# Low parts of K's weights by an accumulating DMA, and K's third group as Strassen pairs

## The chip, the cores and the metric

The kernel runs on one core of one Trainium2 chip. The metric is device time in microseconds (us), from three runs.

## The reference, cut to what matters

A two-layer decoder trunk over 256 tokens, model width 2048, fp32. After the first layer's output `x`, one projection gives the keys and values of three head groups, which the second layer reads:

```python
def shared_kv(x, g, w_kv):
    B, S, _ = x.shape
    parts = split_cols(rmsnorm(x, g) @ w_kv, [DIL_W] * (2 * len(DIL_CONFIG)))   # K0 V0 K1 V1 K2 V2, 2048 columns each
    return [t.reshape(B, S, DIL_HEADS, DIL_DH) for t in parts]
```

So the change lies in one matrix product: 256 tokens by 2048, times 2048 by 12288, in six blocks of 2048 columns. The rest (projections, retention, attention, gates, norms) stays as it is.

## The kernel before, in words

Every fp32 product is made from rounded halves. A tile of 128 x 1024 weights is loaded into `raw`; ACT (ScalarE) writes its rounded high part `wh` (line L97), DVE (VectorE) the rest, `wl = raw - wh` (L98); TensorE multiplies both with the activations' halves. `wh` and `wl` have five buffers each (`SPL = 5`), given out in turn, `raw` has six. SP issues the loads; POOL (GpSimd) issues the DMAs to and from scratch in DRAM (`spill`, `fetch`).

K and V are made in what is called the mixed stage here. K has 12 chunks of 512 columns, each by `dense_cols`: two column halves `i`, in each four weight tiles `j`, in each tile eight times a matmul over 512 columns with `wh` (L315) and one over 256 columns with `wl` (L317): channels come out on the partitions. V is made in pairs of chunks by `strassen`, seven products of quarter blocks instead of eight. A pair is a generator of 28 steps; a step makes one product tile: DVE adds blocks of weights where needed (L361), ACT and DVE split the result, and TensorE does six matmuls over 512 columns (L371 to L373), tokens on the partitions. After certain tiles of K, `weave(n)` runs n steps of the generators in `woven`: (2, 2, 1, 0) after the four tiles of a half and 3 after its eviction. In the stage K's sums live in one accumulator, `acc0`; Strassen's in `acc1` and `acc2`. Small jobs wait in `pending`, and `step()` runs a piece of one of them.

The order on each engine is set by a list scheduler when the kernel is built, with a priority for each instruction; `tc.high_priority(AHEAD)` moves instructions to the front. Each engine then runs its own list strictly in that order and waits on semaphores. The pieces of lists below are its result.

The combinations of activations that Strassen needs (`combine`) are made beside K's first chunk, in which nothing is woven. The scaled activations `yk` (for K and V) and later `yb` (for layer 2) share their source tiles `src`, which stay in SBUF through the stage.

Of the kernel before, what the change touches and what calls it, by code (L numbers as in the profile page):

```python
# [9 lines left out]
F32 = mybir.dt.float32  # L10
F32R = mybir.dt.float32r
AF = mybir.ActivationFunctionType
ALU = mybir.AluOpType
# [8 lines left out]
AHEAD = 100  # L22
# [6 lines left out]
def yoco_trunk_kernel(  # L29
# [8 lines left out]
    pe, act, dve, pool, sp = nc.tensor, nc.scalar, nc.vector, nc.gpsimd, nc.sync  # L38
# [10 lines left out]
    woven = deque()  # L49

    def big_tile(dt=F32):
        return big.tile([P, 4, 256], dt, name="big")
# [16 lines left out]
    def flat(t):  # L69
        return t.rearrange("p a b -> p (a b)")  # L70
# [13 lines left out]
    def acc_tile(name=None):  # L84
        if name is None:
            name = ("acc0", "acc1")[0 if woven else turns["acc"] % 2]
            turns["acc"] += 1
        return psum.tile([P, 2, 2, S], F32, name=name)
# [16 lines left out]
    pending = deque()  # L105
# [9 lines left out]
    def drain():  # L115
        while pending:
            step()

    def weave(n=1):
        for _ in range(n):  # L120
            while woven:
                try:
                    next(woven[0])
                    break
                except StopIteration:
                    woven.popleft()
# [122 lines left out]
    def split_weights(raw, g, k0, n, wh, wl):  # L249
        with tc.high_priority(AHEAD):  # L250
            if g is None:
                split(wh, wl, raw)
                return
            w = 1024 // n
            for i in range(n):
                cs = slice(i * w, (i + 1) * w)
                gs = gain[:, g, k0 + i:k0 + i + 1]
                act.activation(wh[:, cs], raw[:, cs], AF.Copy, scale=gs)
                dve.scalar_tensor_tensor(wl[:, cs], raw[:, cs], gs, wh[:, cs].bitcast(F32), ALU.mult, ALU.subtract)

    def weights(src, g, k0, n, keep=False):
        raw = wraw.tile([P, 1024], F32, name="raw")
        sp.dma_start(out=raw, in_=src)
        if keep:
            wh, wl = flat(big_tile(F32R)), flat(big_tile(F32R))
        else:
            wh = wspl.tile([P, 1024], F32R, name="wh")
            wl = wspl.tile([P, 1024], F32R, name="wl")
        split_weights(raw, g, k0, n, wh, wl)
        w = 1024 // n  # L270
        return [(wh[:, i * w:(i + 1) * w], wl[:, i * w:(i + 1) * w]) for i in range(n)]

# [30 lines left out]
        for i in range(2):  # L303
            evict(i, ps[i])

    def dense_cols(xs, w, c, evict, g=None):
        for i in range(2):
            ps = acc_tile()
            for j in range(4):
                part = xs[j]  # L310
                for a, (wh, wl) in enumerate(weights(w[c, i, j], g, 4 * j, 4)):
                    first, last = j == 0 and a == 0, j == 3 and a == 3
                    for ct in range(2):
                        cs = slice(ct * P, (ct + 1) * P)
                        pe.matmul(ps[:, ct].rearrange("p h s -> p (h s)"), lhsT=wh[:, cs], rhs=xhl(part, a),  # L315
                                  start=first, stop=False, skip_group_check=True)
                        pe.matmul(ps[:, ct, 0, :], lhsT=wl[:, cs], rhs=xh(part, a),  # L317
                                  start=False, stop=last, skip_group_check=True)
                    if a % 2:
                        step()  # L320
                weave((2, 2, 1, 0)[j])
            if woven:
                with tc.high_priority(2 * AHEAD):
                    evict(i, ps)
                weave(3)
            else:
                evict(i, ps)

# [102 lines left out]
    def dense(xs, w, c, g=None, order=(0, 1, 2, 3), both=None, after=None):  # L431
        pt = acc_tile().rearrange("p t h s -> p t (h s)")
        ps = [pt[:, t, :] for t in range(2)]
        n = 4 * len(order)
        k = 0
        late = []

        def row_part(t, part, a, wh, wl, first, last):
            ts = slice(t * P, (t + 1) * P)
            pe.matmul(ps[t], lhsT=xh(part, a)[:, ts], rhs=wh, start=first, stop=False)  # L440
            pe.matmul(ps[t], lhsT=xh(part, a)[:, ts], rhs=wl, start=False, stop=False)  # L441
            pe.matmul(ps[t], lhsT=xl(part, a)[:, ts], rhs=wh, start=False, stop=last)  # L442

        for j in order:
            if len(order) > 4 and j == order[-1]:
                drain()
            part = xs[j]
            for u in range(2):
                keep = both is not None and k >= both
                for a, (wh, wl) in enumerate(weights(w[c, j, u], g, 4 * j + 2 * u, 2, keep), 2 * u):  # L450
                    first, last = k == 0, k == n - 1
                    k += 1
                    row_part(0, part, a, wh, wl, first, last)
                    if keep:
                        late.append((1, part, a, wh, wl, first, last))
                    else:
                        row_part(1, part, a, wh, wl, first, last)
                    step()
                    if len(order) > 4 and k % 2 == 0:
                        step()  # L460
        if after is not None:
            after(ps[0])
        for args in late:
            row_part(*args)
        return ps
# [22 lines left out]
        dense_cols(*job[:3], evict, *job[3:])  # L488
        return h, l

    def cols_scaled(b, *job):
        o = big_tile()

        def evict(i, ps):
            fold(half(o, i), ps)
            if b is not None:
                scale_half(o, i, b)

        dense_cols(*job[:3], evict, *job[3:])
        return o  # L500

    def scale_half(o, i, b):
# [7 lines left out]
    def rows_scaled(ps, r):  # L510
        o = rows(big_tile())
        for t in range(2):
            act.activation(o[:, t, :], ps[t], AF.Copy, scale=r[:, t:t + 1])
        return o
# [230 lines left out]
    def turn_cols(xr, yt):  # L745
        for i in range(2):
            ps = bank()
            for ct in range(2):
                for t in range(2):
                    cs = slice((2 * i + ct) * P, (2 * i + ct + 1) * P)  # L750
                    pe.transpose(ps[:, ct * S + t * P:ct * S + (t + 1) * P], xr[:, t, cs], ident)
            act.copy(half(yt, i), ps)
            yield
# [24 lines left out]
    def spill(t):  # L778
        d = dram.tile([P, 1024], F32, name=f"spill{turns['spill']}")
        turns["spill"] += 1  # L780
        pool.dma_start(out=d, in_=t)
        return d

    def fetch(d):
        t = big_tile()
        pool.dma_start(out=flat(t), in_=d)
        return t

    n_m, n_x = Norm("m"), Norm("x")
    ms = SplitCols(memt, GM)  # L790
    xs = SplitCols(xt, GA)
# [26 lines left out]
    mk0 = big_tile()  # L818
    dense_cols_first(ms, memt, w_mk[0, 0:1], lambda i, ps: fold(half(mk0, i), ps))
    pending.append(stats_m())  # L820
    mk1 = cols_scaled(None, ms, w_mk[0], 1)
    drain()
    for i in range(2):
        scale_half(mk1, i, n_m.b)
# [29 lines left out]
    yk, yb = Scaled(GK), Scaled(GB)  # L854
# [20 lines left out]
        dve.memset(o, v)  # L875
        setattr(n_y, f, o)

    comb = {}

    def make_y():  # L880
        ss = small.tile([P, 2], F32, name="ss")
        dve.tensor_reduce(ss, part, AX.X, ALU.add)
        n_y.rstd(ss)
        yield
        for c in range(4):
            for t in range(2):
                act.activation(x1[c][:, t, :], x1[c][:, t, :], AF.Copy, scale=n_y.r[:, t:t + 1])
            yield
            yk.src[c] = yb.src[c] = big_tile()
            yield from turn_cols(x1[c], yk.src[c])  # L890
            yield from yk.start(c)

    pending.append(make_y())
    mk_b = [spill(flat(cols_scaled(n_m.b, ms2, w_mk[1], c))) for c in range(2)]
    mv_b = [spill(rows_scaled(dense(ms2, w_mv[1], c), n_m.r).rearrange("p t c -> p (t c)")) for c in range(2)]
    drain()
    kd, vd = {}, {}

    def done(p):
        def f(o1, o2):  # L900
            for n, o in ((2 * p, o1), (2 * p + 1, o2)):
                vd[n // 4, n % 4] = spill(o.rearrange("p t c -> p (t c)"))
        return f

    pending.append(combine(yk.raw, comb))
    for i in range(3):
        for hg in range(4):
            kd[i, hg] = spill(flat(cols_plain(yk, w_kc, 4 * i + hg)))
            if not kd.keys() - {(0, 0)}:
                drain()  # L910
                for p in range(6):
                    woven.append(strassen(yk, comb, w_vs[p], done(p)))
    while woven:
        weave()

# [11 lines left out]
        yield  # L927

    for j in range(4):
        pending.append(yb.start(j))  # L930
    mix = SplitMix()
    for c in range(2):
# [163 lines left out]
```

## Time and profile before

| | |
|---|---|
| runs | 1897.88, 1902.02, 1902.39 us; median 1902.02 |
| profiled execution, its own time | 1899.93 us |
| its span, first to last instruction | 1898.2 us |
| TensorE busy, share of the span | 1875.5 us, 99% |
| VectorE | 1317.7 us, 69% |
| ScalarE | 985.8 us, 52% |
| granted TensorE clock | 1.00 in every stage |

A matmul's listed duration (400 ns for 512 columns) overlaps with its neighbours', so what one costs is read from the distance between starts in the timeline, and a "99% busy" TensorE can still hold short waits. A tile's name without its buffer number (`wl`, `big`) stands for all its buffers.

### The profile page before, as it was taken

The numbers are of one execution on the slowest core, as the hardware profiler recorded it, in microseconds if no ns is written. First come the engines' busy times: TensorE is split into PE (matmuls) and PEld (weight loads), VectorE is DVE, ScalarE is ACT, GpSimd is POOL, SyncE is SP. The second block draws the span as 40 slices with busy tenths as digits, with TensorE's granted clock in tenths as the row PEclk, the third lists the DMA queues.
The fourth block names the chain that finished last, engine by engine and source line by source line (L and its number), as shares of the span: only waits on it lengthen the run. The fifth ranks groups of instructions, "written<-read, shape, count | busy, mean of one in ns | idle before, by whom it ended". The sixth has DMA issues, their size and how long they took to land.

```text
span 1898.2 us, 25963 instructions
## 1 busy us (share of the span) xinstructions
PE 1875.5 (99%) x9988; PEld 1604.6 (85%) x9988; DVE 1317.7 (69%) x1571; ACT 985.8 (52%) x1288; POOL 47.5 (3%) x88
## 2 busy tenths in 40 slices
PE   8999999999999999999999999999999999999997
PEld 7888888888888888888888888788889898888886
DVE  7766765665564757899999999866657475656643
ACT  6554445444454645555655556554545454545543
POOL 1000000000000000000000000000000000000000
PEclk9999999999999999999999999999999999999999
DMA  9654565565676666575766667666655556566462
GB/s 304 234 167 157 162 202 180 168 202 184 215 253 208 196 213 212 201 251 192 244 211 222 240 203 256 233 222 210 202 187 181 187 160 218 165 207 220 151 199 100
DMA packets 112588, 385.25 MB, mean 203 GB/s; under 512 B 12385, under 2 KB 18577, under 8 KB 112465
## 3 DMA queue, kind: packets, MB, share of 16 engines
q1 hardware_dynamic: 102784, 349.22, 56.5%
q0 software_dynamic: 9536, 34.37, 5.0%
q8 instruction: 78, 1.28, 0.3%
q14 instruction: 46, 0.37, 0.1%
q10 hardware_dynamic: 144, 0.01, 0.0%
HBM read 364.68 MB, written 18.87 MB: 202 GB/s over the span
## 4 chain that ended last, share of the span: by engine, by line
PE 93%; DVE 2%; issue 2%; ACT 1%; DMA 1%; SPq 0%; POOL 0%; ACTq 0%; POOLq 0%; DVEq 0%
PE acc L315 33%; PE acc L317 17%; PE acc L440 9%; PE acc L441 9%; PE acc L442 9%; PE acc L371 4%; PE acc L372 4%; PE acc L373 4%; DVE wl L98 1%; PE att L102 1%; PE att L103 1%; PE att L101 1%; PE acc L298 1%; ACT wh L97 1%; PE att L714 1%
## 5 line engine op out<-in xcount | busy, mean ns | idle before, releaser
L98 DVE TENSOR_TENSOR wl<-raw,wh 128x1024 fp32r<-128x1024 f32 (+1 forms) x642 | 769.3, 1209 | 461.8 <-ACT wh L97 459.9
L97 ACT CAST wh<-raw 128x1024 fp32r<-128x1024 f32 (+1 forms) x642 | 660.4, 1040 | 673.8 <-PE acc L315 263.6
L315 PE MATMUL acc<-big,wh 128*128 128x512 f32 x2752 | 983.5, 400 | 5.6 <-DVE big L221 2.4
L317 PE MATMUL acc<-big,wl 128*128 128x256 f32 x2752 | 771.3, 280 | 0.8 <-DVE wl L98 0.8
L315 PEld LDWEIGHTS acc<-big,wh 128*128 128x128 f32 x2752 | 517.8, 188 | 127.7 <-DVE big L470 3.1
L317 PEld LDWEIGHTS acc<-big,wl 128*128 128x128 f32 x2752 | 520.2, 189 | 5.0 <-DVE wl L98 1.1
L440 PE MATMUL acc<-wh,big 128*128 128x512 f32 x744 | 291.6, 392 | 0.0
L441 PE MATMUL acc<-wl,big 128*128 128x512 f32 x744 | 289.8, 390 | 0.0
L442 PE MATMUL acc<-wh,big 128*128 128x512 f32 x744 | 289.8, 390 | 0.0
L442 PEld LDWEIGHTS acc<-wh,big 128*128 128x128 f32 x744 | 139.7, 188 | 29.1
L440 PEld LDWEIGHTS acc<-wh,big 128*128 128x128 f32 x744 | 139.8, 188 | 28.2
L441 PEld LDWEIGHTS acc<-wl,big 128*128 128x128 f32 x744 | 139.8, 188 | 27.8
L371 PE MATMUL acc<-wh,big 128*128 128x512 f32 x336 | 133.2, 397 | 1.2 <-ACT wh L97 1.0
L372 PE MATMUL acc<-wl,big 128*128 128x512 f32 x336 | 131.7, 392 | 0.5 <-DVE wl L98 0.5
L373 PE MATMUL acc<-wh,big 128*128 128x512 f32 x336 | 131.6, 392 | 0.0
L97 ACT CAST wh<-big 128x1024 fp32r<-128x1024 f32 x72 | 75.5, 1049 | 72.5 <-DVE big L361 57.7
L98 DVE TENSOR_TENSOR wl<-big,wh 128x1024 fp32r<-128x1024 f32 x72 | 87.8, 1220 | 19.3 <-ACT wh L97 19.1
L371 PEld LDWEIGHTS acc<-wh,big 128*128 128x128 f32 x336 | 63.1, 188 | 17.1 <-ACT wh L97 1.7
L373 PEld LDWEIGHTS acc<-wh,big 128*128 128x128 f32 x336 | 63.1, 188 | 14.8
L372 PEld LDWEIGHTS acc<-wl,big 128*128 128x128 f32 x336 | 63.2, 188 | 11.8 <-DVE wl L98 1.0
L361 DVE TENSOR_TENSOR big<-big,raw 128x1024 f32<-128x1024 f32 x48 | 58.5, 1219 | 0.3
L98 DVE TENSOR_TENSOR big<-big 128x512 fp32r<-128x512 f32 (+1 forms) x54 | 43.4, 823 | 4.6 <-ACT big L97 3.2
(230 smaller groups left out, 1264.5 us busy)
## 6 DMA issues: line engine op xcount, KB each, us to landing
raw<-in_w_b_dram SPq DMA_DIRECT2D x160, 512.0 KB, 3.5
raw<-in_w_kc_dram SPq DMA_DIRECT2D x96, 512.0 KB, 4.4
raw<-in_w_vs_dram SPq DMA_DIRECT2D x96, 512.0 KB, 4.5
raw<-in_w_ac_dram SPq DMA_DIRECT2D x64, 512.0 KB, 3.5
raw<-in_w_ar_dram SPq DMA_DIRECT2D x64, 512.0 KB, 3.9
raw<-in_w_oa_dram SPq DMA_DIRECT2D x48, 512.0 KB, 3.5
raw<-in_w_ob_dram SPq DMA_DIRECT2D x48, 512.0 KB, 3.5
raw<-in_w_mv_dram SPq DMA_DIRECT2D x32, 512.0 KB, 3.5
```

Source lines behind the costliest of these rows:

```text
L97: act.copy(hi, src)
L98: dve.tensor_tensor(lo, src, hi.bitcast(F32), ALU.subtract)
L101: pe.matmul(o, lhsT=ah, rhs=bh, start=first, stop=False, skip_group_check=True)
L315: pe.matmul(ps[:, ct].rearrange("p h s -> p (h s)"), lhsT=wh[:, cs], rhs=xhl(part, a), start=first, stop=False, skip_group_check=True)
L317: pe.matmul(ps[:, ct, 0, :], lhsT=wl[:, cs], rhs=xh(part, a), start=False, stop=last, skip_group_check=True)
L361: f(*args)
L371: pe.matmul(ps, lhsT=h, rhs=wh[:, cs], start=first, stop=False, skip_group_check=True)
L372: pe.matmul(ps, lhsT=h, rhs=wl[:, cs], start=False, stop=False, skip_group_check=True)
L373: pe.matmul(ps, lhsT=l, rhs=wh[:, cs], start=False, stop=last, skip_group_check=True)
L440: pe.matmul(ps[t], lhsT=xh(part, a)[:, ts], rhs=wh, start=first, stop=False)
L441: pe.matmul(ps[t], lhsT=xh(part, a)[:, ts], rhs=wl, start=False, stop=False)
L442: pe.matmul(ps[t], lhsT=xl(part, a)[:, ts], rhs=wh, start=False, stop=last)
```

## The change

It has four parts. (1) While Strassen steps are woven in, a K tile's low part is no longer made by DVE: ACT writes `wh`, ACT writes `wl = -wh` (L272 of the changed kernel), and a DMA from POOL's queue adds the weights, read from DRAM once more, onto `wl` in SBUF (L273). (2) K's third group, four of the twelve chunks, becomes two more Strassen pairs; their output has tokens on the partitions, so each of their four chunks is turned by eight 128 x 128 transposes on TensorE (`turn_out`, a pending job) and then spilled. (3) The order: `combine` moves ahead into V's second chunk of layer 2's memory projection, the generators start with K's first chunk, eight K chunks run beside eight pairs, and the weaves become (4, 4, 3, 0) and 4. (4) `yk.src` is spilled and fetched again for `yb` behind the stage; one accumulator is named `acc2` early in the kernel.

```diff
-        split_weights(raw, g, k0, n, wh, wl)
+        if woven:
+            with tc.high_priority(AHEAD):
+                act.copy(wh, raw)
+                act.activation(wl, wh.bitcast(F32), AF.Copy, scale=-1.0)
+                pool.dma_start(out=wl, in_=src, accum_op=ALU.add)
+        else:
+            split_weights(raw, g, k0, n, wh, wl)
...
-                weave((2, 2, 1, 0)[j])
+                weave((4, 4, 3, 0)[j])
             if woven:
                 with tc.high_priority(2 * AHEAD):
                     evict(i, ps)
-                weave(3)
+                weave(4)
...
-    mk1 = cols_scaled(None, ms, w_mk[0], 1)
+    mk1 = cols_scaled(None, ms, w_mk[0], 1, name="acc2")
...
-            yk.src[c] = yb.src[c] = big_tile()
+            yk.src[c] = big_tile()
             yield from turn_cols(x1[c], yk.src[c])
+            yd.append(spill(flat(yk.src[c])))
             yield from yk.start(c)
...
+    for c in range(2):
+        if c == 1:
+            pending.append(combine(yk.raw, comb))
+        mv_b.append(spill(rows_scaled(dense(ms2, w_mv[1], c), n_m.r).rearrange("p t c -> p (t c)")))
...
+    def turn_out(o, key):
+        t = big_tile()
+        yield from turn_cols(o, t)
+        kd[key] = spill(flat(t))
...
-                vd[n // 4, n % 4] = spill(o.rearrange("p t c -> p (t c)"))
+                if n < 12:
+                    vd[n // 4, n % 4] = spill(o.rearrange("p t c -> p (t c)"))
+                else:
+                    pending.append(turn_out(o, (2, n % 4)))
...
-    pending.append(combine(yk.raw, comb))
-    for i in range(3):
+    for p in (0, 1, 6, 2, 3, 7, 4, 5):
+        woven.append(strassen(yk, comb, w_vs[p], done(p)))
+    for i in range(2):
         for hg in range(4):
             kd[i, hg] = spill(flat(cols_plain(yk, w_kc, 4 * i + hg)))
-            if not kd.keys() - {(0, 0)}:
-                drain()
-                for p in range(6):
-                    woven.append(strassen(yk, comb, w_vs[p], done(p)))
...
     for j in range(4):
+        yb.src[j] = fetch(yd[j])
         pending.append(yb.start(j))
```

What this does to the lists, at three places in the middle of the mixed stage. A row is a line of the code, an operation, the tile written, the tiles read, the width, and the kind of semaphore waited on. First TensorE, before: the end of one K tile (`wl_8601`), one Strassen step, and the start of the next K tile, `wl_8644`.

```order
L315 MATMUL acc0_8502<-big_5605,wh_8600 128x512
L317 MATMUL acc0_8502<-big_5605,wl_8601 128x256
L371 MATMUL acc1_6389<-wh_8631,big_6235 128x512 [waits Activation_49]
L372 MATMUL acc1_6389<-wl_8632,big_6235 128x512 [waits DVE_49]
L373 MATMUL acc1_6389<-wh_8631,big_6235 128x512
L371 MATMUL acc1_6389<-wh_8631,big_6235 128x512
L372 MATMUL acc1_6389<-wl_8632,big_6235 128x512
L373 MATMUL acc1_6389<-wh_8631,big_6235 128x512
L315 MATMUL acc0_8502<-big_5689,wh_8643 128x512 [waits Activation_49]
L317 MATMUL acc0_8502<-big_5689,wl_8644 128x256 [waits DVE_49]
L315 MATMUL acc0_8502<-big_5689,wh_8643 128x512
```

TensorE, after (L315, L317 and L371 to L373 are now L321, L323 and L377 to L379). The row just ahead of these is the last that reads the K tile `wl_8871`; its buffers are the ones that `wh_8951` and `wl_8952`, five tiles on, will get.

```order
L379 MATMUL acc2_6214<-wh_8929,big_6013 128x512
L377 MATMUL acc2_6214<-wh_8929,big_6013 128x512
L378 MATMUL acc2_6214<-wl_8930,big_6013 128x512
L379 MATMUL acc2_6214<-wh_8929,big_6013 128x512
L377 MATMUL acc1_6213<-wh_8939,big_6052 128x512
L378 MATMUL acc1_6213<-wl_8940,big_6052 128x512 [waits DVE_49]
L379 MATMUL acc1_6213<-wh_8939,big_6052 128x512
L377 MATMUL acc1_6213<-wh_8939,big_6052 128x512
L378 MATMUL acc1_6213<-wl_8940,big_6052 128x512
L379 MATMUL acc1_6213<-wh_8939,big_6052 128x512
L321 MATMUL acc0_8796<-big_5610,wh_8951 128x512 [waits Activation_49]
L323 MATMUL acc0_8796<-big_5610,wl_8952 128x256 [waits DMASW5_49]
```

The first use of `wl` now waits for a DMA of POOL's queue (DMASW) where it waited for DVE. Between the last read of the old owner and the first read of `wl_8952` stand eleven matmuls.

Second ACT, around the same K tiles; before, one copy for each tile:

```order
L97 CAST wh_8600<-raw_8598 128x1024 [waits DMAHW1_49,DVE_49,PE_49]
L97 CAST wh_8631<-raw_8622 128x1024 [waits DVE_49,PE_49,Activation_49]
L97 CAST wh_8643<-raw_8641 128x1024 [waits DMAHW5_49,PE_49,Activation_49]
L97 CAST wh_8665<-big_8626 128x1024 [waits PE_49,Activation_49]
L97 CAST wh_8675<-raw_8624 128x1024 [waits DMAHW4_49,PE_49,Activation_49]
L97 CAST wh_8685<-raw_8620 128x1024 [waits DMAHW2_49,PE_49,Activation_49]
```

and after, with the copy (L271) and the negation (L272) of the K tiles:

```order
L433 COPY big_8358<-acc2_6214 128x512 [waits DVE_49,PE_49]
L271 CAST wh_8951<-raw_8949 128x1024 [waits DMAHW6_49,DVE_49]
L272 ACTIVATE wl_8952<-wh_8951 128x1024 [waits DMASW0_49,Activation_49]
L97 CAST wh_8972<-raw_8908 128x1024 [waits DMAHW3_49,DVE_49,PE_49]
L97 CAST wh_8993<-raw_8984 128x1024 [waits DVE_49,PE_49]
L97 CAST wh_9003<-big_8988 128x1024 [waits PE_49]
L271 CAST wh_9015<-raw_9013 128x1024 [waits DMAHW2_49,PE_49]
L272 ACTIVATE wl_9016<-wh_9015 128x1024 [waits Activation_49]
```

Each K tile now has two rows on ACT, and other tiles' copies behind them. Third POOL, the same stretch; before it held only spills:

```order
L781 DMA spill19_8401<-big_7748 128x1024 [waits DMASW7_49,DVE_49]
L781 DMA spill18_8399<-big_7747 128x1024 [waits DMASW0_49,Activation_49]
L781 DMA spill20_8695<-big_8305 128x1024 [waits DMASW1_49,DVE_49]
L781 DMA spill23_9080<-big_8697 128x1024 [waits DMASW2_49,DVE_49]
L781 DMA spill22_9078<-big_8426 128x1024 [waits DMASW3_49,DVE_49]
```

and after, the accumulating DMAs (L273) stand between them in one list:

```order
L787 DMA spill25_8904<-big_8359 128x1024 [waits DMASW2_49,DVE_49]
L273 DMA wl_8871<-in_w_kc_dram 128x1024 [waits DMASW1_49,PE_49,Activation_49]
L787 DMA spill24_8902<-big_8358 128x1024 [waits DVE_49,Activation_49]
L273 DMA wl_8952<-in_w_kc_dram 128x1024 [waits DMASW0_49,DMASW5_49,PE_49,Activation_49]
L273 DMA wl_9016<-in_w_kc_dram 128x1024 [waits DVE_49,PE_49,Activation_49]
L787 DMA spill26_9089<-big_8512 128x1024 [waits DVE_49]
L273 DMA wl_9096<-in_w_kc_dram 128x1024 [waits DMASW6_49,PE_49,Activation_49]
```

There are 60 such DMAs in the stage; four of K's 64 tiles come after the last Strassen step and keep DVE's subtraction.

## Rows read from the trace of the kernel before

**Rows 1.** The page: span, busy time, share of the span and instructions of each engine.

```profile
span 1898.2 us, 25963 instructions
...
PE 1875.5 (99%) x9988; PEld 1604.6 (85%) x9988; DVE 1317.7 (69%) x1571; ACT 985.8 (52%) x1288; POOL 47.5 (3%) x88
```

**Rows 2.** Windows, 720 to 1227 us: busy us (instructions) by engine, clock, DMA share, GB/s.

```profile
720.00:1227.00 507.00, 504.89 (x2545) 423.81 (x2543) 470.19 (x453) 290.14 (x319) 12.79 (x24) 1.00 0.67 224
```

**Rows 3.** Waits, 717 to 1212 us: who waited for whom; total us, times, longest us.

```profile
ACT wh L97 <- DVE raw L361: 85.0, 22, 6.2
...
ACT wh L97 <- PE acc L373: 15.9, 20, 3.1
...
PEld acc L371 <- ACT wh L97: 1.7, 2, 0.9
...
PE acc L372 <- DVE wl L98: 0.5, 1, 0.5
```

**Rows 4.** Timeline of PE: start us, us, engine, line, operation, tiles, shape, count.

```profile
719.97 0.39 PE L315 MATMUL acc<-big,wh 128*128 128x512 f32 x1
...
1210.82 0.40 PE L371 MATMUL acc<-wh,big 128*128 128x512 f32 x1
...
1213.34 0.39 PE L373 MATMUL acc<-wh,big 128*128 128x512 f32 x1
...
1214.38 0.39 PE L315 MATMUL acc<-big,wh 128*128 128x512 f32 x1
...
1217.55 0.40 PE L315 MATMUL acc<-big,wh 128*128 128x512 f32 x1
...
1226.58 0.28 PE L317 MATMUL acc<-big,wl 128*128 128x256 f32 x1
```

**Rows 5.** Groups by line, 717 to 1212 us: count, busy us, mean ns, idle before.

```profile
L98 DVE TENSOR_TENSOR wl<-raw,wh 128x1024 fp32r<-128x1024 f32 x187 | 221.2, 1219 | 12.1 <-ACT wh L97 11.1
...
L97 ACT CAST wh<-raw 128x1024 fp32r<-128x1024 f32 x187 | 189.5, 1049 | 113.5 <-DVE raw L361 85.0 <-PE acc L315 9.1 <-PE acc L373 7.9
...
L361 DVE TENSOR_TENSOR big<-big,raw 128x1024 f32<-128x1024 f32 x48 | 58.5, 1219 | 0.3
...
L470 DVE TENSOR_TENSOR big<-acc,big 128x512 f32<-128x512 f32 x22 | 15.0, 684 | 1.2 <-ACT big L469 1.2
...
L416 DVE TENSOR_TENSOR big<-big,acc 128x512 f32<-128x512 f32 x15 | 9.5, 680 | 0.1
```

**Rows 6.** The chain that ended last, 630 to 640 us: start us, us, engine, line.

```profile
633.94 0.44 PE att L751 x4
```

**Rows 7.** Timeline of ACT in the stage before, 700 to 722 us.

```profile
703.85 1.05 ACT L97 CAST wh<-raw 128x1024 fp32r<-128x1024 f32 x1 [1.67 <-PE acc L442]
706.57 1.05 ACT L97 CAST wh<-raw 128x1024 fp32r<-128x1024 f32 x1 [1.67 <-PE acc L442]
709.29 1.05 ACT L97 CAST wh<-raw 128x1024 fp32r<-128x1024 f32 x1 [1.67 <-PE acc L442]
```

**Rows 8.** Groups by line and shape, the whole run: a plain copy and a scaled one.

```profile
L97 ACT CAST big<-sm 128x512 fp32r<-128x512 f32 x20 | 12.3, 616 | 11.4 <-DVE sm L470 11.4
...
L540 ACT ACTIVATE sm<-big 128x512 f32<-128x512 f32 x16 | 10.1, 629 | 8.4 <-DVE big L473 8.4
```

**Rows 9.** DMA queues and issues, 717 to 1212 us; packets, MB, share; count, KB, landing us.

```profile
q1 hardware_dynamic: 26754, 97.41, 60.0%
q0 software_dynamic: 3168, 11.54, 6.0%
...
raw<-in_w_kc_dram SPq DMA_DIRECT2D x88, 512.0 KB, 4.5
spill<-big POOLq DMA_DIRECT2D x22, 512.0 KB, 5.1
```

**Rows 10.** DMA issues, 898 to 901 and 829 to 840 us: a quick and a slow spill.

```profile
spill<-big POOLq DMA_DIRECT2D x1, 512.0 KB, 2.8
...
spill<-big POOLq DMA_DIRECT2D x1, 512.0 KB, 6.9
```

More of the change, by code (lines that the diff above doesn't have):

```diff
@@ L304, in dense_cols_first, with dense_cols @@
             evict(i, ps[i])
-    def dense_cols(xs, w, c, evict, g=None):
+    def dense_cols(xs, w, c, evict, g=None, name=None):
         for i in range(2):
-            ps = acc_tile()
+            ps = acc_tile(name if i == 0 else None)
             for j in range(4):
@@ L489, in cols_plain2, with cols_scaled @@
         return h, l
-    def cols_scaled(b, *job):
+    def cols_scaled(b, *job, name=None):
         o = big_tile()
@@ L497, in evict @@
                 scale_half(o, i, b)
-        dense_cols(*job[:3], evict, *job[3:])
+        dense_cols(*job[:3], evict, *job[3:], name=name)
         return o
@@ L876, in yoco_trunk_kernel @@
         setattr(n_y, f, o)
-    comb = {}
+    comb, yd = {}, []
     def make_y():
@@ L894, in yoco_trunk_kernel @@
     mk_b = [spill(flat(cols_scaled(n_m.b, ms2, w_mk[1], c))) for c in range(2)]
-    mv_b = [spill(rows_scaled(dense(ms2, w_mv[1], c), n_m.r).rearrange("p t c -> p (t c)")) for c in range(2)]
+    mv_b = []
+    for c in range(2):
+        if c == 1:
+            pending.append(combine(yk.raw, comb))
+        mv_b.append(spill(rows_scaled(dense(ms2, w_mv[1], c), n_m.r).rearrange("p t c -> p (t c)")))
     drain()
     kd, vd = {}, {}
+    def turn_out(o, key):
+        t = big_tile()
+        yield from turn_cols(o, t)
+        kd[key] = spill(flat(t))
     def done(p):
@@ L1076 @@
         "w_mv": np.stack([rblocks(cat(w_mem_kv[i], (1024, 2048))) for i in range(2)]),
-        "w_kc": cblocks(cat(w_kv, (0, 2048), (4096, 6144), (8192, 10240))),
-        "w_vs": sblocks(cat(w_kv, (2048, 4096), (6144, 8192), (10240, 12288))),
+        "w_kc": cblocks(cat(w_kv, (0, 2048), (4096, 6144))),
+        "w_vs": sblocks(cat(w_kv, (2048, 4096), (6144, 8192), (10240, 12288), (8192, 10240))),
         "g_a": col_gain(norm_a[0]), "g_b": col_gain(norm_b[0]), "g_mem": col_gain(mem_norm_g), "g_kv": col_gain(kv_norm_g),
```

## The prediction

> **What bounds the kernel now.** I read the page first. TensorE is busy for 1875.5 of 1898.2 us and DVE for 69% [rows 1], so time is won only where TensorE does less or waits less. Then I read the stage that is changed. K's first matmul starts at 719.97 us and its last at 1226.58 [rows 4], a stage of 507 us. In it DVE is busy for 470 us, ACT for 290, and the DMA engines for 67% [rows 2]: DVE is the next limit, at 93%. The waits say the same: ACT's copies wait 85 us for DVE's sums of weights, while TensorE's own waits are 1.7 and 0.5 us [rows 3]. So before the change TensorE sets the pace and DVE follows closely.
>
> The cost of a matmul is the distance between starts. Eleven steps of Strassen's 512 columns take 2.52 us, 0.229 us each; nine pairs of a K tile (512 and 256 columns) take 3.17 us, 0.352 each [rows 4]. A K chunk is 64 pairs, 22.5 us; a Strassen pair is 28 x 6 = 168 matmuls, 38.5 us at that pace. Twelve chunks and six pairs make 501 us, within 6 us of the stage as it ran; that small rest is waits and hops between the two kinds.
>
> **The change, part by part.** *TensorE's work.* Four chunks go (-90.0 us), two pairs come (+77.0). The four chunks that come out turned need eight groups of four transposes; the trace has such a group at 0.44 us [rows 6], so +3.6 us. Net -9.4 us: about 492 us where the stage now has 501, plus its rest.
>
> *DVE.* It loses the low parts of K and gains those of two pairs. By its rows (1.22 us for a split or a sum, 0.68 for a half-width piece [rows 5]): 224 splits 273 us, 128 sums 156, four K tiles at the end 5, sixteen evictions 11, 64 combinations of products 44: 489 us against 492 on TensorE. It neither improves nor clearly breaks.
>
> *ACT.* 60 more passes. A scaled pass of 512 columns takes 629 ns where a plain one takes 616 [rows 8], so over 1024 columns I take the plain copy's 1.05 us [rows 5]: +63 us, and 56 more plain copies of product tiles less 32 of K, +25. ACT stays under 400 of 492 us. As busy time all this is hidden; as latency it isn't.
>
> *The new chain.* What decides is how long a K tile's low part takes, counted from the moment when its buffer is free. ACT really does run at that edge: in the stage before, three copies in a row each start on TensorE's release of a buffer [rows 7]. Before, a freed buffer needed a copy (1.05) and a subtraction (1.22): 2.3 us. After, it needs a hop (0.1), the copy (1.05), the negation (1.05), in 37 of the 60 tiles another tile's copy between these two (1.05), and then the DMA.
>
> How long may it take? With the weaves (4, 4, 3, 0) and 4, a half has 4 K tiles and 15 steps, and five buffers. Three of the four K tiles get the buffers of the K tile just before, with four steps between: 24 x 0.23 = 5.5 us. Counted row by row in the changed lists, 44 of the 60 tiles inherit from a K tile, with 5.8 us of TensorE work on average between the last read of the old and the first read of the new low part (2.5 us at the place shown above); the other 16 have 8.0. Before, the same count gives hardly any tile under 5.7, for a need of 2.3.
>
> *The DMA's price.* No DMA before accumulates. The nearest rows are DMAs of the same 512 KB in this stage: loads on SP's queue land 4.5 us after issue, spills on POOL's queue 5.1 [rows 9]; single spills go from 2.8 to 6.9 [rows 10]. An accumulating one also reads its destination. If that doubles its transfer, it adds 1.6 us: 109 MB took 66% of 495 us [rows 9], so the engines at full share move 334 GB/s, and 0.524 MB takes 1.6 us. I take 5.5 us, POOL's own median and a little for the read, and keep 2.8 and 6.9 as ends.
>
> The Trainium skill, "DMA: Bandwidth & Descriptors", section "Anatomy of one DMA — SWDGE (gpsimd) path", gives such a transfer as about 2.0 us plus its bytes at 436 GB/s, an estimate of 3.2 us here; by it the waits below would be 32 us and the kernel 1923 us. The trace's median of 5.1 us for this size and queue disagrees, its quickest, 2.8, does not.
>
> *The sum.* Need: 0.1 + 2.1 + 0.65 (the copy between, on average) + 5.5 = 8.35 us. Tiles that inherit from K: 44 x (8.35 - 5.8) = 112 us; the 16 others overrun by little. Tile by tile, adding only what is positive, it is 117 us at 5.5; 22 us at 2.8; 40 at 3.5; 100 at 5.1; 178 at 6.9. TensorE takes its list in order, so these waits add up: they lie one behind the other. Behind the waiting row stand the next Strassen steps, and with them DVE and ACT, which then have time to spare: no second stall is added. POOL's spills stand in the same list (the last of the pieces shown with the change) and wait for evictions; that can only make a low part later, and I leave it at nothing.
>
> *The rest.* `combine` moves into a stage where DVE was not short (the chunk it leaves had nothing woven); it costs nothing. The four fetches of `yb`'s source stand behind the last accumulating DMA, and TensorE has over 20 us of work between that tile and the first use of `yb`; at up to 7 us they are hidden. The extra spills are 0.53 us each on an idle engine. The name `acc2` is worth at most a wait of an eviction, about 1 us.
>
> Against the profiled execution: 1899.9 - 9.4 + 117 = 2007.5. The median shown is 2 us above that execution, so 2010.
>
> **The rivals.** *The DMA engines become the bound.* The stage would move 64 K loads, 60 accumulating reads, 128 loads for Strassen and about 25 spills, 145 MB, 435 us of the engines at 334 GB/s; with the destination read too, 60 x 0.524 = 31 MB more, 529 us, over TensorE's 492. Then landings stretch beyond 7 us: 2075 us at 6.9, 2200 at 10. For it: 67% now [rows 2], and 4.5 us for loads under this load. Against it: the waits themselves lengthen the stage and thin the traffic. The Trainium skill, "Collectives: The Full Stack", section "The bandwidth ceiling: the fold count and why AG ≠ RS ≠ AR", says that a DMA that adds reads two sources and so runs at about half rate, which speaks for this; no run so far shows it.
>
> *The chain is hidden after all, and the kernel is faster.* The low part would have to land within about 2 us of issue (waits of 9 us, as much as is won); then it is 1890 us. Against it: no DMA of this size in the rows lands under 2.8.
>
> *The chain is hidden, but DVE decides.* At 489 us of DVE work, run at the 93% of now, the stage would last 527 us: +20. Between no loss and that, 1895 to 1920. For it: ACT's 85 us of waits for DVE [rows 3].
>
> **How the numbers follow.** The chain as summed, landings of 3.5 to 7 us, 1930 to 2080: 0.70. DMA engines as the bound, above that: 0.13. Hidden and faster: 0.07. Hidden with DVE deciding, or landings near 3 us, 1895 to 1930: 0.10, about half of it within 0.3% of 1902. 0.3% is about what a measurement of this kernel can tell from no change. Faster 0.08, the same 0.05, slower 0.87. The range is 1905 to 2110: it leaves 0.12 below and about 0.08 above.
>
> **What would show it.** The mixed stage from about 507 us to 580 to 680, all other stages as they were. TensorE idle before L323 (first use of `wl`) on POOL's DMAs, some 40 times, 2 to 3 us each. Landings of the accumulating DMAs at 5 to 6 us. DVE's share in the stage down to about 80%. I am wrong if these landings are under 3 us, if TensorE's waits on them sum to under 30 us, or if the lost time stands in front of Strassen's rows, waiting for DVE.

## The result, and the profile after

The changed kernel takes 2101.57 us (median of 4 runs, 2097.20 to 2107.46) beside 1901.58 of the kernel before in the same comparison: 1.1058 times as long, with an interval of [1.1024, 1.1091]. Its profiled execution, the slowest of the four, has a span of 2105.6 us. The direction of the prediction held, and the time lies inside its range, 8 us below the upper end; the loss is 200 us where 108 were forecast.

First the page, which answers to [rows 1]: busy time and its share, then the queue of POOL's DMAs over the whole span.

```profile
span 2105.6 us, 25863 instructions
...
PE 1932.9 (92%) x9844; PEld 1629.6 (77%) x9844; DVE 1324.3 (63%) x1575; ACT 1073.2 (51%) x1378; POOL 104.0 (5%) x156
...
q0 software_dynamic: 19328, 70.03, 13.5%
```

TensorE has 144 instructions fewer and is busy 57 us longer: the same kind of work has become slower. Its idle time went from 22.7 us (1898.2 less 1875.5) to 172.7. The windows say where; the mixed stage is the second row and answers to [rows 2].

```profile
0.00:719.00 719.00, 711.68 (x3621) 604.29 (x3622) 460.25 (x595) 371.49 (x513) 18.07 (x35) 1.00 0.63 205
719.00:1430.00 711.00, 555.34 (x2361) 442.79 (x2360) 463.11 (x433) 370.50 (x395) 67.11 (x87) 0.90 0.70 202
1430.00:2105.00 675.00, 665.88 (x3865) 582.52 (x3863) 400.97 (x548) 331.24 (x471) 18.78 (x35) 1.00 0.57 192
```

The stage takes 711 us instead of 507, which is the whole loss; the time ahead of it is the same, and the time behind it within 4 us. In the stage TensorE is idle for 156 us, DVE's share falls to 65%, and the granted clock to 0.90. The waits of TensorE in the stage, which answer to [rows 3] (total us, times, longest us):

```profile
PE acc L323 <- DMA wl<-in_w_kc_dram: 137.7, 43, 7.1
PE acc L377 <- ACT wh L97: 3.6, 3, 2.2
PE acc L377 <- DVE big L411: 2.9, 3, 1.2
PE acc L377 <- DVE big L422: 2.9, 4, 1.5
```

The DMA issues of the stage, which answer to [rows 9], and from the view of line L273 the spread of the accumulating ones:

```profile
raw<-in_w_vs_dram SPq DMA_DIRECT2D x123, 512.0 KB, 4.7
raw<-in_w_kc_dram SPq DMA_DIRECT2D x62, 512.0 KB, 4.9
wl<-in_w_kc_dram POOLq DMA_DIRECT2D x59, 512.0 KB, 7.3
...
DMA to landing us min/median/max: 5.4/7.3/10.4
```

Of the 156 us, 138 stand in front of the first use of a low part, in 43 of the 60 tiles, 3.2 us each; all other waits are small. An accumulating transfer lands 7.3 us after issue, a load of the same size 4.7 to 4.9.

One such wait, step by step. The timelines (start, us, engine, line, operation, tiles; in brackets the idle time ahead and what ended it) of ACT, of POOL and of TensorE around one K tile:

```profile
805.07 1.05 ACT L271 CAST wh<-raw 128x1024 fp32r<-128x1024 f32 x1 [4.18 <-PE acc L321]
...
809.34 1.06 ACT L272 ACTIVATE wl<-wh 128x1024 fp32r<-128x1024 f32 x1
```

```profile
811.00 0.89 POOL L273 DMA_DIRECT2D wl<-in_w_kc_dram  x1 [1.68 <-ACT wl L272]
```

```profile
813.91 0.39 PE L379 MATMUL acc<-wh,big 128*128 128x512 f32 x1
821.42 0.58 PE L323 MATMUL acc<-big,wl 128*128 128x256 f32 x1 [7.12 <-DMA wl<-in_w_kc_dram]
821.80 0.63 PE L321 MATMUL acc<-big,wh 128*128 128x512 f32 x1
822.23 0.41 PE L323 MATMUL acc<-big,wl 128*128 128x256 f32 x1
822.44 0.63 PE L321 MATMUL acc<-big,wh 128*128 128x512 f32 x1
...
825.53 0.40 PE L321 MATMUL acc<-big,wh 128*128 128x512 f32 x1
825.76 0.28 PE L323 MATMUL acc<-big,wl 128*128 128x256 f32 x1
825.88 0.39 PE L377 MATMUL acc<-wh,big 128*128 128x512 f32 x1
```

ACT's copy starts when TensorE has released the buffer (L321). Two evictions and two copies of other tiles stand between it and the negation, which starts 4.3 us later; 0.6 us after the negation's end POOL issues the DMA, at 811.00. It lands 10.4 us later, the slowest of the stage, and TensorE, which was there at 814.3, waits 7.1 us. On average over the 60 tiles it is 1.95 us from the copy's start to the negation's, 1.06 for the negation, 0.35 from its end to the issue and 7.2 to the landing: 10.6 us.

The rows behind the wait show a second loss, of which the prediction had nothing: a pair of matmuls (L321 and L323) starts 0.64 us after the pair ahead of it, until 825.0; the next step is 0.53 us, and from 825.5 on it is 0.35. The windows of the wait, of the slow rows and of those behind give the granted clock (the last column but two) and the DMA engines' share behind it (a packet counts whole in the window in which it starts, so the share can pass 1):

```profile
814.30:821.40 7.10, 0.00 (x0) 0.00 (x0) 2.96 (x4) 4.35 (x5) 0.90 (x1) 0.80 1.04 342
821.40:825.00 3.60, 3.58 (x11) 3.10 (x12) 3.46 (x3) 0.00 (x0) 0.00 (x0) 0.50 1.06 297
825.50:830.00 4.50, 4.50 (x23) 3.73 (x22) 2.95 (x3) 3.16 (x3) 0.00 (x0) 1.00 0.41 125
```

After a wait of 7 us TensorE runs 3.6 us at half its clock, 1.2 GHz for 2.4. The Trainium skill describes just this, in "TensorE: Matmul & The Clock Gate", section "HAM oscillation — how this bites in real kernels": a kernel whose TensorE waits for DMAs again and again runs part of its time at the lower clock. The trace agrees (0.50 here, 0.90 over the stage). And while the transfer is under way, the DMA engines are full (1.04).

### The profile page after: what moved, and what is told of

Its sections match the earlier page's. It is cut to its first block, busy times and chain, and to the rows that moved or that the text cites. A ratio compares the mean times of both kernels' runs of the same rounds, so it can differ in the third digit from the quotient of the medians.

```text
span 2105.6 us, 25863 instructions
## 1 busy us (share of the span) xinstructions
PE 1932.9 (92%) x9844; PEld 1629.6 (77%) x9844; DVE 1324.3 (63%) x1575; ACT 1073.2 (51%) x1378; POOL 104.0 (5%) x156
## 3 DMA queue, kind: packets, MB, share of 16 engines
q0 software_dynamic: 19328, 70.03, 13.5%
## 5 line engine op out<-in xcount | busy, mean ns | idle before, releaser
L98 DVE TENSOR_TENSOR wl<-raw,wh 128x1024 fp32r<-128x1024 f32 (+1 forms) x582 | 701.2, 1209 | 519.0 <-ACT wh L97 517.5
L97 ACT CAST wh<-raw 128x1024 fp32r<-128x1024 f32 (+1 forms) x582 | 602.9, 1038 | 671.1 <-PE acc L321 308.2
L321 PE MATMUL acc<-big,wh 128*128 128x512 f32 x2496 | 934.2, 414 | 6.5 <-DVE big L476 2.6
L323 PE MATMUL acc<-big,wl 128*128 128x256 f32 x2496 | 726.4, 291 | 137.7 <-DMA wl<-in_w_kc_dram 137.7
L323 PEld LDWEIGHTS acc<-big,wl 128*128 128x128 f32 x2496 | 494.3, 198 | 156.9 <-DMA wl<-in_w_kc_dram 155.7
L321 PEld LDWEIGHTS acc<-big,wh 128*128 128x128 f32 x2496 | 491.1, 197 | 122.3 <-DVE big L221 2.6
L446 PE MATMUL acc<-wh,big 128*128 128x512 f32 x744 | 291.7, 392 | 0.0
L448 PE MATMUL acc<-wh,big 128*128 128x512 f32 x744 | 290.0, 390 | 0.0
L447 PE MATMUL acc<-wl,big 128*128 128x512 f32 x744 | 289.8, 389 | 0.0
L377 PE MATMUL acc<-wh,big 128*128 128x512 f32 x448 | 179.3, 404 | 12.6 <-ACT wh L97 3.6
L378 PE MATMUL acc<-wl,big 128*128 128x512 f32 x448 | 178.9, 399 | 2.6 <-DVE wl L98 2.4
L379 PE MATMUL acc<-wh,big 128*128 128x512 f32 x448 | 177.0, 395 | 0.0
L98 DVE TENSOR_TENSOR wl<-big,wh 128x1024 fp32r<-128x1024 f32 x96 | 117.3, 1222 | 74.1 <-ACT wh L97 73.8
L448 PEld LDWEIGHTS acc<-wh,big 128*128 128x128 f32 x744 | 139.7, 188 | 29.1
L446 PEld LDWEIGHTS acc<-wh,big 128*128 128x128 f32 x744 | 139.8, 188 | 27.9
L377 PEld LDWEIGHTS acc<-wh,big 128*128 128x128 f32 x448 | 86.0, 192 | 38.2 <-ACT wh L97 6.7
L379 PEld LDWEIGHTS acc<-wh,big 128*128 128x128 f32 x448 | 86.0, 192 | 18.2
L271 ACT CAST wh<-raw 128x1024 fp32r<-128x1024 f32 x60 | 62.8, 1047 | 69.8 <-PE acc L321 40.7
L273 POOL DMA_DIRECT2D wl<-in_w_kc_dram x60 | 52.6, 876 | 535.1 <-ACT wl L272 393.1
```

The lines of the kernel that those rows point to most:

```text
L97: act.copy(hi, src)
L98: dve.tensor_tensor(lo, src, hi.bitcast(F32), ALU.subtract)
L271: act.copy(wh, raw)
L273: pool.dma_start(out=wl, in_=src, accum_op=ALU.add)
L377: pe.matmul(ps, lhsT=h, rhs=wh[:, cs], start=first, stop=False, skip_group_check=True)
L378: pe.matmul(ps, lhsT=h, rhs=wl[:, cs], start=False, stop=False, skip_group_check=True)
```

## The experiments

Every kernel was timed in three rounds, beside the kernel before on the same chip. Times are medians; ratios are to the kernel before, with a 95% interval.

### What the stage takes without K's low parts

K's low parts are left out in the first of two kernels: neither negation nor DMA, and the second matmul reads `wh` again. The pairs, turns, order and spills of the change stay.

```diff
...
-                act.activation(wl, wh.bitcast(F32), AF.Copy, scale=-1.0)
-                pool.dma_start(out=wl, in_=src, accum_op=ALU.add)
+            wl = wh
```

> The changed kernel without K's low parts in the stage: no negation, no DMA, and the low matmuls read the high part again (so K's first two groups get a wrong small term; all of TensorE's work stays). Theory (TensorE's work alone is 9 us less than before, DVE's 489 us fit beside it): 1888 to 1900 us. Rival (DVE or the weaves' order hold the stage at DVE's old share of 93%): 1905 to 1925 us.

It took 1912.84 us, 1.0069 [1.0048, 1.0089]: nothing is waited for on POOL's queue, and still it is slower than before. Its ACT waits in the stage:

```profile
ACT wh L97 <- DVE big L366: 85.7, 29, 5.7
ACT wh L97 <- DVE raw L366: 71.1, 22, 5.5
```

ACT stands behind DVE's sums of weights, as in [rows 3], and passes the delay on to TensorE in small pieces. The second kernel takes that work from DVE as well (the lines of the first kernel are left out here):

```diff
...
-            ahead(dve.tensor_tensor, s1, w11, w12, ALU.add)
-            ahead(dve.tensor_tensor, w12, w12, w22, ALU.add)
-            ahead(dve.tensor_tensor, s2, s1, w22, ALU.add)
+            ahead(act.copy, s1, w11)
+            ahead(act.copy, s2, w22)
...
-            ahead(dve.tensor_tensor, s2, s2, w21, ALU.add)
```

> The kernel of e8 (K's low parts left out: 1912.8) with Strassen's sums of the weights left out as well: two of them are copies by ACT instead, the others are gone, so DVE has some 150 us less to do in the mixed stage and ACT some 65 more; the result is not the reference's. Theory 1, VectorE's work sets the mixed stage of e8 and hides TensorE's 9 us of gain: 1886 to 1899. Theory 2, the order in which the Strassen rows are woven between the chunks does: within 8 us of e8, 1905 to 1920.

It took 1890.67 us, 0.9955 [0.9940, 0.9970], 8 us less than the kernel before. Two windows, the first 508 us of the stage and 100 us late in it, first of the kernel with the sums:

```profile
719.00:1227.00 508.00, 492.45 (x2328) 401.91 (x2329) 451.17 (x423) 302.49 (x333) 13.33 (x25) 0.99 0.63 219
1100.00:1200.00 100.00, 99.49 (x483) 81.57 (x482) 93.84 (x89) 64.33 (x72) 4.80 (x9) 1.00 0.70 236
```

and of the one without:

```profile
719.00:1227.00 508.00, 502.24 (x2431) 417.07 (x2430) 331.61 (x327) 381.52 (x411) 16.84 (x32) 1.00 0.67 230
1100.00:1200.00 100.00, 100.00 (x489) 83.65 (x489) 64.26 (x62) 75.26 (x82) 4.25 (x8) 1.00 0.70 247
```

With the sums DVE is busy for 94% late in the stage, as it was over the stage before the change ([rows 2], 93%). TensorE loses little in that window (483 matmuls for 489); over the 508 us it is idle for 15.6 us with the sums and for 5.8 without, and does 103 matmuls fewer. Without the sums TensorE's 9 us of saved work appear. The sums on DVE cost 22 us once nothing else is in the way. Their work went together with the waits of other rows for their results, so what each of the two costs is not told apart.

### The pairs with DVE's subtraction kept

```diff
-        if woven:
-            with tc.high_priority(AHEAD):
-                act.copy(wh, raw)
-                act.activation(wl, wh.bitcast(F32), AF.Copy, scale=-1.0)
-                pool.dma_start(out=wl, in_=src, accum_op=ALU.add)
-        else:
-            split_weights(raw, g, k0, n, wh, wl)
+        split_weights(raw, g, k0, n, wh, wl)
```

> The changed kernel with DVE's subtraction for every low part, no accumulating DMA; pairs, turns, weaves and order as changed. Theory (the chain copy, negation, DMA is too long for five buffers): TensorE's 138 us of waits on these DMAs are gone and its clock stays up; what is left is DVE, with 489 + 60 x 1.22 = 562 us of work in the stage, which then sets it: 560 to 600 us, total 1955 to 1995 us. Rival (the third group as pairs, the turns or the new weaves cost the time): about as slow as the changed kernel, over 2040 us.

It took 1958.56 us, 1.031 [1.029, 1.033], as the theory of DVE's work said. A window of the stage and some 20 us behind it:

```profile
719.00:1300.00 581.00, 540.61 (x2483) 426.73 (x2483) 543.79 (x524) 318.88 (x354) 17.59 (x33) 0.98 0.61 209
```

DVE is busy for 544 of these 581 us, 94%, where TensorE has 492 us of work in the stage by the prediction's count: the third group as pairs costs DVE more than it saves TensorE. So the two halves of the change need each other, and the kernel that keeps DVE's subtraction is still 143 us quicker than the one that gives it to the DMA.

### The accumulating DMA alone

The kernel before with nothing but the new low part, in the 85 of K's tiles beside which Strassen steps run:

```diff
-        split_weights(raw, g, k0, n, wh, wl)
+        if woven:
+            with tc.high_priority(AHEAD):
+                act.copy(wh, raw)
+                act.activation(wl, wh.bitcast(F32), AF.Copy, scale=-1.0)
+                pool.dma_start(out=wl, in_=src, accum_op=ALU.add)
+        else:
+            split_weights(raw, g, k0, n, wh, wl)
```

> The kernel before with the accumulating DMA alone (12 chunks of K, 6 pairs, old weaves and order). Theory: 85 tiles go through the chain, with 7.2 us of TensorE work on average between a buffer's release and its next use against a need of about 9.7 us; waits of about 220 us and a lower clock, 2100 to 2180 us. Rival (pairs, turns or weaves are the cost, the DMA is not): within 20 us of 1902.

It took 2079.55 us, 1.093 [1.089, 1.098], a little under the range and nowhere near the rival. TensorE's longest wait in total from 719 to 1300 us:

```profile
PE acc L323 <- DMA wl<-in_w_kc_dram: 104.5, 57, 4.4
```

and the issues in the same stretch:

```profile
raw<-in_w_vs_dram SPq DMA_DIRECT2D x89, 512.0 KB, 5.9
raw<-in_w_kc_dram SPq DMA_DIRECT2D x74, 512.0 KB, 5.1
wl<-in_w_kc_dram POOLq DMA_DIRECT2D x74, 512.0 KB, 7.6
```

The loss is that of the new low part, negation and accumulating DMA, whatever is done about K's third group. The waits were not as expected: 124 us over the whole run, where 220 were counted; TensorE's busy time rose by 52 us beside them. Here the other loads become slower too (5.9 us for Strassen's), with the DMA engines at 85% in this stretch.

### A plain transfer in the same place

```diff
-                pool.dma_start(out=wl, in_=src, accum_op=ALU.add)
+                pool.dma_start(out=wl, in_=src)
```

> The changed kernel with a plain DMA of the same weights onto the negated high part instead of an accumulating one (same queue, size, order and waits; the sum is left out, so the low parts are wrong by the high part). Theory (the chain, of which the addition is a part): landing 5 to 5.5 us instead of 7.3, software queue at the rate of spills instead of half; by the count of the lists waits fall from about 230 to 105 to 125 us, and the total to 1985 to 2020 us. Rival (any DMA of POOL's queue is as slow, the addition costs nothing): within 15 us of 2101.

It took 2020.75 us, 1.063 [1.060, 1.067]: 81 us less than the changed kernel, just above the upper end of what the theory gave, and far from the rival. TensorE's first wait in the stage:

```profile
PE acc L323 <- DMA wl<-in_w_kc_dram: 71.1, 43, 5.9
```

and, from its page, the queue over the whole span and the landing:

```profile
q0 software_dynamic: 19328, 70.03, 10.1%
...
wl<-in_w_kc_dram POOLq DMA_DIRECT2D x60, 512.0 KB, 4.9
```

The same bytes on the same queue take 10.1% of 2010.3 us, 203 us of the engines' time, where the accumulating ones took 13.5% of 2105.6, 284 us. At the plain rate (70.03 MB in 203 us, 345 GB/s) the 60 transfers of 31.5 MB are 91 us; accumulating, they are 172, an estimate that leaves the queue's other transfers at the same time in both. So adding onto the destination nearly halves the rate, to some 183 GB/s. The Trainium skill has the same ratio for the adding transfers of a ring collective, in "Collectives: The Full Stack", section "The bandwidth ceiling: the fold count and why AG ≠ RS ≠ AR": the add needs two source reads, and the rate is about half. This trace agrees, for a transfer of one core from DRAM onto SBUF (172 us against 91). By the other rule of the Trainium skill that the prediction weighed, "DMA: Bandwidth & Descriptors", section "Anatomy of one DMA — SWDGE (gpsimd) path", the landing was an estimate of 3.2 us; the trace has 4.9 even for the plain one.

### Buffers of K's own

If the low part is late because its buffer comes free late, buffers that only K uses should help. Two `big` tiles and one pair of the shared `wh` and `wl` buffers make room.

```diff
-BIG = 30
-SPL = 5
+BIG = 28
+SPL = 4
+KSPL = 2
...
+        elif woven:
+            wh = kspl.tile([P, 1024], F32R, name="kh")
+            wl = kspl.tile([P, 1024], F32R, name="kl")
```

> The changed kernel with two pairs of buffers of their own for K's tiles in the stage, four instead of five for the others, and 28 big tiles instead of 30. A K tile now gets the buffer of the K tile before the last: 11.7 us of TensorE work on average between release and use. Theory (buffers): most waits go, about 25 us left at a landing of 7.3 us; 1890 to 1930 us. Rival (the DMA engines are the bound: they work for 498 us in the changed kernel's stage, 0.70 of 711): the stage can't get under 540 us or so, landings grow past 9 us, 1940 us or more.

With three each instead of two (`BIG = 26`):

> As the run with two, but three pairs of buffers for K's tiles and 26 big tiles: 19.6 us on average between release and use. Theory (buffers): no wait on these DMAs up to a landing of 12 us; DVE's 489 us beside TensorE's 492 sets what is left, 1890 to 1910 us. Rival (DMA engines): 1940 us or more, as with two.

They took 2022.12 us, 1.064 [1.061, 1.067], and 2021.37, 1.063 [1.061, 1.066]. Buffers brought 79 us, and the theory that they alone were short fell: the third pair brought nothing. The rival's sign didn't show either: the landings were 7.1 and 7.6 us, not past 9. The kernel with three, waits of all engines from 719 to 1300 us:

```profile
ACT kh L276 <- DMA raw<-in_w_kc_dram: 96.2, 28, 6.3
...
PE acc L328 <- DMA kl<-in_w_kc_dram: 71.8, 21, 6.8
```

The wait has moved one link up: ACT now has a buffer, and waits for the weights themselves, because K's tiles take their turn among the six `raw` tiles. The same with a plain transfer:

> Three pairs of buffers of their own for K's tiles, and the plain DMA (the sum left out). Theory (DMA engines as the second limit, which the run with three own pairs showed): their work in the stage falls by some 86 us, from about 498 to 412 of 492, landings to about 5.5 us, and the loads come sooner; 1905 to 1950 us. Rival (the rest of the run with own buffers is something else: the order on ACT, the six raw tiles): little under 2021, over 1980 us.

1968.98 us, 1.037 [1.035, 1.039], between the two expectations: 52 us come from the transfer, and the wait for `raw` is still there (84.6 us, 30 times). So K was given two raw tiles of its own as well, beside two high and two low ones:

```diff
-        raw = wraw.tile([P, 1024], F32, name="raw")
+        raw = kraw.tile([P, 1024], F32, name="kr") if woven else wraw.tile([P, 1024], F32, name="raw")
```

> The changed kernel, accumulating, with two pairs of own buffers for K's tiles and two raw tiles of their own for K beside the six (26 big tiles). Theory (DMA engines at half rate for the addition): loads can be issued earlier, but the engines have 498 us to do; 1980 to 2020 us. Rival (raw tiles: ACT's copies of K waited 99 us for K's raw loads in the run with three own pairs, because the load could not be issued earlier): these waits go, 1950 us or less.

1978.01 us, 1.041 [1.039, 1.043], just below the theory's range and well above the rival's: the raw tiles brought 44 us over the kernel with two pairs. In all 124 us of the changed kernel's 200 are gone, with the same accumulating DMA. And with a plain one:

> The kernel of e6 (two buffers each for K's high and low parts, two raw tiles of K's own) with a plain DMA in place of the accumulating one; the sum is left out, so K's low parts are wrong. Theory 1, the accumulating transfer takes the DMA engines' time (half rate) and lands late: e6's 1978 falls by the 46.8 us that it waited for the landing, less some waits that stay, to 1915 to 1945, with the landing at 5 us or below and the DMA share near 0.7. Theory 2, what is left in e6 is the order of the engines' work (ACT's parts behind TensorE's groups): 1960 to 1980.

1936.53 us, 1.020 [1.018, 1.021], as the first theory said. TensorE's waits in the stage of this kernel, to 1250 us:

```profile
PE acc L330 <- DMA kl<-in_w_kc_dram: 18.8, 14, 2.6
PE acc L385 <- DVE wl L102: 12.9, 8, 3.2
```

It is 24 us above the kernel without low parts, which has one negation and one DMA less for each tile.

### Work for TensorE in the place of its waits

Six matmuls that nobody reads stand ahead of each of the 60 K tiles:

```diff
+                    if woven and a == 0:
+                        fill = psum.tile([P, 512], F32, name="att", bufs=2)
+                        for _ in range(6):
+                            pe.matmul(fill, lhsT=wh[:, 0:P], rhs=xhl(part, 0), start=True, stop=True, skip_group_check=True)
```

> The changed kernel (2101.6) with six matmuls of 512 columns, into a bank that nobody reads, ahead of each of the 60 K tiles of the mixed stage: about 1.4 us of TensorE work a tile, 83 us in all, that ends before the low part is needed. Theory 1, some 50 us of the loss is TensorE at the lower clock after its waits: the filler lies where TensorE waited in 43 tiles, the granted clock of the stage rises from 0.90 to over 0.95, and the time is 2060 to 2095. Theory 2, the clock costs little, or the waits only move behind the filler: 2105 to 2185.

2130.26 us, 1.121 [1.119, 1.124]: theory 1 missed, and the time lies in the range of theory 2. Its page:

```profile
span 2128.4 us, 26566 instructions
...
PE 1999.6 (94%) x10204; PEld 1691.0 (79%) x10204; DVE 1324.8 (62%) x1575; ACT 1074.4 (50%) x1378; POOL 104.3 (5%) x156
```

TensorE's wait in the stage, and a window of its first 531 us:

```profile
PE acc L327 <- DMA wl<-in_w_kc_dram: 106.5, 45, 5.3
```

```profile
719.00:1250.00 531.00, 452.33 (x1969) 366.66 (x1968) 337.97 (x314) 269.61 (x286) 47.28 (x60) 0.92 0.69 196
```

The filler is 60 times 1.36 us (the distance from its first start to the next kind's), 82 us. TensorE is busy only 67 us longer, so its other work became 15 us quicker, and it is idle 44 us less (128.8 instead of 172.7): 82 - 15 - 44 = 23 us more, which is what the span shows. The clock gave back a little, the waits gave back about half of what was put into them, and the sum is a loss.

## Why the prediction was right, and where its sizes were off

The kernels without low parts and without sums, without low parts, with own buffers, and the changed one run 9844 instructions on TensorE each, so their pages can be set side by side (profiled executions, us; the granted clock is the mean of the run):

| kernel | span | TensorE busy | idle | granted clock |
|---|---|---|---|---|
| no low parts, no sums | 1890.6 | 1867.5 | 23.1 | 0.996 |
| no low parts | 1912.0 | 1877.8 | 34.2 | 0.994 |
| own buffers and raw, plain DMA | 1936.4 | 1880.7 | 55.7 | 0.994 |
| own buffers and raw, accumulating | 1978.5 | 1895.9 | 82.6 | 0.984 |
| changed kernel, plain DMA | 2010.3 | 1900.6 | 109.7 | 0.986 |
| changed kernel | 2105.6 | 1932.9 | 172.7 | 0.965 |

The changed kernel is 215 us above the first row: 149.6 of idle time and 65.4 in which the same number of instructions took longer. The prediction had 1890.5 + 117 + 0.

- **TensorE's work, -9.4 us: right.** With everything else out of the way the kernel is 8 us quicker than before, and its TensorE is busy for 8 us less (1867.5 for 1875.5).
- **DVE neither improves nor clearly breaks: it would have broken.** At 489 us of work against 492 it costs 22 us where nothing waits for the DMA; the kernel without low parts, at 1913, lies in the 1895 to 1920 of the rival that had DVE decide. In the changed kernel this doesn't show, since TensorE's waits give DVE time (65% busy).
- **The place of the loss: right.** 43 waits in front of the first use of `wl`, where 44 tiles were counted, on POOL's DMA; the other stages stayed as they were; combine, fetches and spills cost nothing that the windows show.
- **The landing, 5.5 us: mis-sized, the first step that failed.** It measured 7.3, over the upper end of 6.9. The prediction put the read of the destination at little; it costs 81 us in the time of the kernel (plain against accumulating), by its own rate and by the load that it puts on the DMA engines. The rival of the DMA engines named that mechanism and forecast times from 2075 up; the time lies there. (By the prediction's own table the rival's times are 2070 at a landing of 6.9 and, with 3.1 us more in each of 60 tiles, some 2255 at 10, not 2075 and 2200.) It was half of the matter: the engines are full in stretches (1.04 above) but at 70% over the stage, and with a plain transfer 119 us of loss remain.
- **The rest of the need, and the time that covers it: both counted too short.** From the copy's start to the landing 10.6 us pass, where the sum had 8.25; the landing is 1.7 of the difference, the steps ahead of it 0.6, above all 0.35 us between the negation and the issue, for which nothing was taken. By the prediction's own table a landing of 7.3 alone would have cost some 200 us of waits, and 4.9 some 92 (between its 40 at 3.5 and 100 at 5.1). Measured were 138 and 71, so the tiles had more time than the 5.8 us counted. That count took a K tile's buffers, three times out of four, to be those of the K tile just ahead, and the trace doesn't bear it out. At the place shown with the change, where `wh_8951` and `wl_8952` were said to get the buffers of `wl_8871` and its high part, ACT's copy and negation of the new tile, and TensorE's last matmul with `wl_8871`, ran at these times (the rows around them are those of the lists, in their order):

```profile
1151.81 1.05 ACT L271 CAST wh<-raw 128x1024 fp32r<-128x1024 f32 x1
1152.89 1.06 ACT L272 ACTIVATE wl<-wh 128x1024 fp32r<-128x1024 f32 x1
```

```profile
1162.08 0.41 PE L323 MATMUL acc<-big,wl 128*128 128x256 f32 x1
```

The new low part is begun 9 us before the old one is read for the last time, so they lie in different buffers, and TensorE didn't wait for this tile. In 31 of the 59 K tiles behind the first, the copy starts ahead of TensorE's last matmul with the K tile before. The 28 others may have its buffers; TensorE comes to their first low matmul 7.7 us after that last one, on average, and 27 of them wait, 95 us in all; the other 16 waits make 43 us. Whose buffers the 31 got, the trace doesn't tell.

- **Waits add up and no second stall is added: wrong, the second step that failed.** No second wait of that size appeared, but TensorE itself became slower, and the 65 us are a third of the result. The changed kernel and the one with a plain DMA have the same TensorE list in the same order, and differ by 32 us of busy time beside 63 of idle time. In the other rows the order differs in places, and the busy time still rises with the idle time from row to row; the filler moved it by 15 us in the other direction. How much of it is the clock can be estimated: the granted clock was 0.50 for 147 us of the changed kernel's run, and TensorE was busy for 118 of these. At the pace of the pairs above (0.35 us for 0.64) that work would have taken 53 us less; the same count gives 5 us in the first row. So some 49 of the 65 us are the clock. The other 16 are not accounted for; a longer first matmul behind each wait (0.58 us at 821.42, where the next of L323 take 0.41 at the same clock) would be 7 of them.

The two errors of the sum, 33 us of idle time (21 in front of the low parts, 12 elsewhere) and 65 us of slower matmuls, make the difference of 98 in the profiled executions; in the medians it is 92. That the range held owes something to luck: the band of 1930 to 2080, which had 0.70, was missed, and what lay above it had 0.13; and a need and a cover that were both too short worked against each other. Of the signs that it named, the place and the number of the waits came (43 of 3.2 us); the stage (711 us, not 580 to 680), the landings (7.3, not 5 to 6) and DVE's share (65%, not 80%) lay outside. No version tried beats the kernel before, except the one that leaves the sums out, which computes something else.

## What to carry to other kernels

A transfer that replaces work of a busy engine brings its latency into a chain that buffers must cover: count the chain from the release of the buffer to the first use, make sure which buffer a tile really gets, and count every shared pool in it, since a buffer added at one link (high and low parts) moves the wait to the next (the raw tiles). When TensorE's waits are many and short, price them above their own length: here each us of idle time came with 0.4 us of slower matmuls (65 for 150). And before moving work off the engine that is second, ask whether it is the limit of the new plan: VectorE was, by 22 us, and the third group as pairs would have brought 9.

## What was not expected of the hardware

- A DMA that adds onto SBUF moves some 183 GB/s while the DMA engines work at it, by the estimate above, where a plain one of the same queue and size moves 345; 512 KB land after 7.3 us instead of 4.9, and its issue occupies POOL for 0.87 us instead of 0.54.
- After a wait of 7 us TensorE's granted clock was 0.50 for 3.6 us, a pair of matmuls 0.64 us instead of 0.35; over a stage with 43 waits of 3.2 us it was 0.90.
